# Splitting parked weights in a two-layer decoder kernel: the low half computed on GpSimd, not on VectorE

## The chip, the cores and the metric

The kernel runs on one NeuronCore of one Trainium2 chip. The core has TensorE (PE, matrix products), VectorE (DVE), ScalarE (ACT), GpSimd (POOL) and the queue engine SyncE (SP), which issues every DMA of this program. The metric is device time in microseconds of one execution, lower is better. The median of three executions of the kernel before is 1376.49 us (1376.41 to 1377.57).

## The reference, cut to what matters

The input is one sequence of 1024 rows with 1024 columns, float32. The first layer is differential attention with 8 heads, the second stick-breaking attention with 16 heads of 64, whose K and V come from a projection of their own:

```python
def reference(x, a_norm, a_w_in, a_w_out, ..., kv_norm, w_kv, b_norm, b_w_in, b_w_out):
    x = _diff_layer(x, pos, a_norm[0], a_w_in[0], a_w_out[0], ...)   # rms norm, q k v g, softmax - lam*softmax,
                                                                     # norm, times silu(g), out projection, plus x
    shared_k, shared_v = _shared_kv(x, kv_norm, w_kv)                # _rms(x, kv_norm) @ w_kv
    return _sb_layer(x, shared_k, shared_v, b_norm[0], b_w_in[0], b_w_out[0])  # _rms(x, b_norm) @ w_in, attention,
                                                                               # times silu(g), @ w_out, plus x

def _rms(x, g):
    y = x * lax.rsqrt(jnp.mean(x * x, axis=-1, keepdims=True) + RMS_EPS)
    return y * g
```

The factors `g` of the norms ahead of the second layer (`kv_norm`, `b_norm`) belong to rows of `w_kv` and `b_w_in`, so the kernel multiplies them into these weights.

## The kernel before, in words

**Products of halves.** Every float32 operand of a product is split into a high half (the value rounded to the matmul's fp32r type) and a low half (value minus high half). A product is then three matmuls: high by high, high by low, low by high. So each weight tile of 128 by 512 has to be split once on the chip: ACT copies it to the high half `h`, and an engine subtracts `h` from the value to get `l`.

**First layer.** The projections for the 8 heads run one head ahead of their attention. For every head the weights `w_qk` and `w_vg` are loaded in eight pieces of 128 by 512 into tiles called `raw`, and split into tiles called `w` (`split_w`, L519). PE multiplies (`proj`). The q and k rows go through ACT (`qk`), a norm on DVE, the rotary embedding on POOL (four instructions on `g1k` and `qk`, L1007), transposes on PE (`tr`), and a split into `q`, `qz`, `kh`, `kl`. Scores (`sc`) are evacuated by DVE to `z`, the softmax is ACT's exponentials and two passes of DVE over `z`, PE transposes the result, and ACT and DVE split it into `th` and `tl` for the product with `v` (`av`). In the last block of a row of blocks, POOL first clears a part of `th` and `tl` (L690). The gate's SiLU uses POOL twice: a bound from below on `g2k` (L610), for which ACT's exponential waits, and a product (L614). At the end come the output projection, whose weights `a_w_out` also pass through `raw` tiles, and the norm's sum of squares, also through `raw`.

**Parking.** In the same layer, spread over the steps of heads 0 to 6 (`extra`, L1195), the second layer's weights are split ahead of time and written to DRAM: 32 tiles of `w_kv`, 32 of `w_b` (both with their norm's factor `gain`) and 16 of `b_w_out` (none). That is `park` (L540): load to `raw`, `h` by ACT, `l` by DVE in place over `raw`, and two DMAs out. The second layer reads the halves back and splits no weights.

**One pool of four.** `raw` has four buffers. Parked tiles (two each, `raw` and `h`), head weights, output weights and sums of squares all take them, strictly in the order in which the code asks for them.

**What sets the order.** Nothing is issued as the code runs. Every operation is recorded, and a planner (`Order.issue`, L271) then lays out one order for all engines from a table of costs (`Order.cost`, L240), priorities and free buffers. An operation under `later()` has a low priority, one under `hp()` the highest. Each engine and the DMA queue of SP then work strictly in that order. All recorded operations carry the line L377 in the profile, so rows are told apart by tile names. The table gives a POOL operation on n columns 0.1 + 0.0028 n, a DVE `scalar_tensor_tensor` 0.12 + 0.00103 n.

Of the kernel before, what the change touches and what calls it, by code (L numbers as in the profile page):

```python
# [17 lines left out]
ALU = mybir.AluOpType  # L18
# [14 lines left out]
def f32(ap):  # L33
    return ap.bitcast(F32)
# [345 lines left out]
def build(tc, ins, out):  # L380
    nc = tc.nc
    rec = Order(tc, {"pe": nc.tensor, "act": nc.scalar, "dve": nc.vector, "pool": nc.gpsimd, "sp": nc.sync})
    act, dve, pool, pe, sp = (rec.engine(e) for e in ("act", "dve", "pool", "pe", "sp"))
# [22 lines left out]
    def later():  # L406
        return rec.priority(B["late"])
# [9 lines left out]
    def T(tag, shape, bufs, dt=F32, pool=None):  # L417
        n_t[0] += 1
        pool, name = pool or "sb", f"{tag}_{n_t[0]}"
        return L(Root(shape, dt, "psum" if pool == "ps" else "sbuf", pool, slot=(pool, tag), bufs=bufs,  # L420
                      make=lambda: pools[pool].tile(shape, dt, tag=tag, bufs=bufs, name=name)))
# [118 lines left out]
    def park(src, gain, dst):  # L540

        with later():
            raw = T("raw", [P, HALF], B["raw"], pool=layer[0])
            h = T("raw", [P, HALF], B["raw"], pool=layer[0]).bitcast(F32R)
            l = raw.bitcast(F32R)
            sp.dma_start(raw, src)
            if gain is None:
                act.activation(h, raw, AF.Copy)
                dve.tensor_tensor(l, raw, f32(h), ALU.subtract)
            else:  # L550
                act.activation(h, raw, AF.Copy, scale=gain)
                dve.scalar_tensor_tensor(l, raw, gain, f32(h), ALU.mult, ALU.subtract)
            for i, t in enumerate((f32(h), raw)):
                sp.dma_start(dst(i), t.rearrange("p (j n) -> p j n", j=2))

# [640 lines left out]
    for p2 in range(4):  # L1196
        for w, dst, c0 in ((w_kv, w2_kv, 16), (w_b, w2_b, 8)):
            for kc in range(KC):
                extra.append(lambda w=w, dst=dst, c0=c0, p2=p2, kc=kc: park(
                    w[p2, kc], cols[:, c0 + kc:c0 + kc + 1],  # L1200
                    lambda i: dst[2 * p2:2 * p2 + 2, i, :, kc * 256:(kc + 1) * 256].rearrange("j p n -> p j n")))
    for c in range(4):
        for g in range(4):
            extra.append(lambda c=c, g=g: park(
                ins["b_w_out"][c, g], None,
                lambda i: w2_o[c, i, :, g * 512:(g + 1) * 512].rearrange("p (j n) -> p j n", j=2)))
# [166 lines left out]
```

## Time and profile before

| | us |
|---|---|
| median of three executions | 1376.49 |
| the profiled execution | 1375.14 |
| its span (first to last instruction) | 1373.4 |
| first layer with parking | about 60 to 590 |
| PE, DVE, ACT, POOL busy in the span | 1334.1, 1134.5, 937.6, 349.6 |

The profiled execution is one run with the hardware's profiler, its own time 1.7 us over its span and 1.35 us under the median of the runs. In rows that group instructions, the form is `out<-in`, the shape out and in, how many, then the busy time, the mean of one in nanoseconds, and the engine's idle time before them with what ended it. PEld is PE's weight load. "SPq" is an issue by SP; its duration is that of the issue, not of the transfer.

### The profile page before, as it was taken

The page shows a single profiled execution, that of the slowest core. Times are in us where ns is not written, and L with a number is a line of the kernel's source. Part 1 is how long each engine was busy: PE and PEld are TensorE (multiplying, and loading weights), DVE is VectorE, ACT ScalarE, POOL GpSimd, SP SyncE. Part 2 cuts the span into 40 slices and gives each one's busy share as a digit, 9 for nine tenths or more (in the row PEclk, how much of TensorE's full clock was granted, in tenths as well). Part 3 has the DMA queues.
Part 4 walks back from the last instruction along what each step waited for, and adds up shares of the span by engine and source line. Part 5 has one row for each costly group of instructions (what it writes and reads, how often), then busy time and mean ns, then how long its engine had stood idle before and what let it go on. Part 6 is the DMA issues. An engine that isn't in the chain of part 4 may idle for free.

```text
span 1373.4 us, 22565 instructions
## 1 busy us (share of the span) xinstructions
PE 1334.1 (97%) x7776; PEld 1161.6 (85%) x7776; DVE 1134.5 (83%) x2079; ACT 937.6 (68%) x1830; POOL 349.6 (25%) x595
## 2 busy tenths in 40 slices
PE   8999999999999999999999999999999999999898
PEld 7998989898988888888788888888888888888677
DVE  7699899989998999976654889898989898989771
ACT  7586767676777676634435779887878788876730
POOL 5423222231312232202201124141414141424100
PEclk9999999999999999999999999999999999999999
DMA  5256656556564656862523213131322222266524
GB/s 193 78 162 191 187 160 206 171 151 195 169 207 140 198 161 178 281 233 85 177 77 130 78 64 106 62 107 63 100 70 92 78 92 78 75 201 238 192 89 141
DMA packets 104514, 194.19 MB, mean 141 GB/s; under 512 B 9936, under 2 KB 44496, under 8 KB 103376
## 3 DMA queue, kind: packets, MB, share of 16 engines
q1 hardware_dynamic: 104400, 192.75, 43.7%
q8 instruction: 62, 1.02, 0.3%
q14 instruction: 52, 0.43, 0.1%
HBM read 119.31 MB, written 65.01 MB: 134 GB/s over the span
## 4 chain that ended last, share of the span: by engine, by line
PE 61%; DVE 21%; ACT 10%; DMA 4%; issue 3%; POOL 1%; SPq 0%; DVEq 0%; ACTq 0%; POOLq 0%
PE proj L377 42%; PE av L377 7%; PE tr L377 7%; DVE z L377 5%; PE sc L377 5%; DVE u4k L377 4%; ACT u4k L377 2%; DVE tl L377 2%; ACT zl L377 1%; DVE w L377 1%; ACT qz L377 1%; DVE raw L377 1%; ACT z L377 1%; DVE v L377 1%; DVE o L377 1%
## 5 line engine op out<-in xcount | busy, mean ns | idle before, releaser
L377 PE MATMUL proj<-ah,w 128*128 128x512 f32 x2016 | 694.5, 399 | 5.2 <-DVE ah L377 2.1
L377 PEld LDWEIGHTS proj<-ah,w 128*128 128x128 f32 x2016 | 379.1, 188 | 82.5 <-DVE w L377 2.4
L377 PE MATMUL proj<-al,w 128*128 128x512 f32 x1008 | 394.9, 392 | 0.2 <-DVE al L377 0.2
L377 PEld LDWEIGHTS proj<-al,w 128*128 128x128 f32 x1008 | 190.2, 189 | 29.9 <-DVE al L377 0.5
L377 PE MATMUL proj<-w,ah 128*128 128x256 f32 x1024 | 195.7, 289 | 1.6 <-ACT ah L377 0.7
L377 DVE TENSOR_TENSOR_SCAN u4k<-zl,u4k 128x768 f32<-128x768 f32 (+4 forms) x96 | 176.3, 1837 | 3.0
L377 ACT ACTIVATE u4k<-u4k 128x768 f32<-128x768 f32 (+4 forms) x192 | 158.1, 844 | 18.0 <-DVE u4k L377 15.8
L377 PEld LDWEIGHTS proj<-w,ah 128*128 128x128 f32 x1024 | 161.6, 192 | 3.7 <-ACT ah L377 0.9
L377 DVE TENSOR_TENSOR tl<-tr,th 128x512 fp32r<-128x512 f32 (+1 forms) x240 | 145.1, 629 | 22.4 <-ACT th L377 18.6
L377 PE MATMUL av<-th,v 128*128 128x256 f32 x640 | 147.0, 284 | 3.3 <-ACT th L377 2.4
L377 PE MATMUL proj<-w,al 128*128 128x256 f32 x512 | 146.0, 285 | 3.4 <-DVE al L377 3.3
L377 ACT ACTIVATE th<-tr 128x512 fp32r<-128x512 f32 (+1 forms) x240 | 125.6, 553 | 22.1 <-PE tr L377 12.4
L377 PE MATMUL av<-tl,v 128*128 128x256 f32 x480 | 128.7, 289 | 11.1 <-DVE tl L377 10.7
L377 ACT ACTIVATE z<-z,min 128x256 f32<-128x256 f32 (+7 forms) x128 | 98.6, 771 | 59.8 <-DVE min L377 59.5
L377 POOL TENSOR_TENSOR o<-o,o 128x512 f32<-128x512 f32 (+1 forms) x56 | 85.9, 1534 | 172.0 <-DVE o L377 169.3
L377 PEld LDWEIGHTS av<-th,v 128*128 128x128 f32 x640 | 111.9, 189 | 13.2 <-ACT th L377 3.6
L377 DVE CUSTOM_DVE_ANT_0 z<-sc,mask_a 128x384 f32<-128x384 f32 (+3 forms) x192 | 102.8, 550 | 14.3 <-PE tr L377 7.5
L377 DVE SCALAR_TENSOR_TENSOR u4k<-zl,u4k 128x768 f32<-128x768 f32 (+4 forms) x96 | 96.2, 1002 | 19.3 <-ACT u4k L377 18.8
L377 PEld LDWEIGHTS av<-tl,v 128*128 128x128 f32 x480 | 90.8, 189 | 21.6 <-DVE tl L377 11.3
L377 PEld LDWEIGHTS proj<-w,al 128*128 128x128 f32 x512 | 98.1, 192 | 4.8 <-DVE al L377 4.8
L377 ACT ACTIVATE zl<-u4k 128x768 f32<-128x768 f32 (+4 forms) x96 | 81.5, 849 | 30.0 <-DVE u4k L377 29.8
L377 ACT ACTIVATE zl<-sc 128x384 f32<-128x384 f32 (+3 forms) x192 | 82.8, 494 | 20.9 <-PE sc L377 17.1
(145 smaller groups left out, 2238.6 us busy)
## 6 DMA issues: line engine op xcount, KB each, us to landing
w_kv<-raw SPq DMA_DIRECT2D x64, 256.0 KB, 2.5
w_b<-raw SPq DMA_DIRECT2D x64, 256.0 KB, 2.6
w<-w_kv SPq DMA_DIRECT2D x32, 512.0 KB, 5.3
w<-w_b SPq DMA_DIRECT2D x32, 512.0 KB, 5.0
w<-w_o SPq DMA_DIRECT2D x24, 512.0 KB, 4.9
q<-qz SPq DMA_DIRECT2D x64, 128.0 KB, 2.3
raw<-in_w_kv_dram SPq DMA_DIRECT2D x32, 256.0 KB, 2.9
raw<-in_w_b_dram SPq DMA_DIRECT2D x32, 256.0 KB, 3.0
```

The source lines that it names most:

```text
L377: getattr(e, method)(*[real(x) for x in a], **{k: real(v) for k, v in kw.items()})
```

## The change

In `park`, the subtraction moves from DVE to POOL. For a tile without a factor that is one instruction for one. For a tile with a factor, one DVE instruction (times `gain`, minus `h`) becomes two on POOL: `raw` times `gain` in place, which must wait until ACT has read `raw` for `h`, and then minus `h`, in place again.

```diff
@@ -546,10 +546,10 @@
             sp.dma_start(raw, src)
             if gain is None:
                 act.activation(h, raw, AF.Copy)
-                dve.tensor_tensor(l, raw, f32(h), ALU.subtract)
             else:
                 act.activation(h, raw, AF.Copy, scale=gain)
-                dve.scalar_tensor_tensor(l, raw, gain, f32(h), ALU.mult, ALU.subtract)
+                pool.tensor_scalar(raw, raw, gain, None, ALU.mult)
+            pool.tensor_tensor(l, raw, f32(h), ALU.subtract)
             for i, t in enumerate((f32(h), raw)):
                 sp.dma_start(dst(i), t.rearrange("p (j n) -> p j n", j=2))
```

The planner sees other costs and other engines, so it lays out the first layer anew: the order of every engine differs from the first parked tile to the output projection. In the second layer the order is the same, apart from buffer numbers.

POOL before, around the second rotary embedding of the third head (`g1k`, `qk`), with the clearing of `th` and `tl`, a gate product (`o`) and a gate bound (`g2k`) behind it:

```order
L377 TENSOR_TENSOR g1k_424_2308<-qk_381_2033,rs_93 128x16x8 x2
L377 TENSOR_TENSOR qk_381_2033<-qk_381_2033,rc_92 128x16x16
L377 TENSOR_TENSOR qk_381_2033<-qk_381_2033,g1k_424_2308 128x16x16
L377 MEMSET th_451_2394 128x128
L377 MEMSET tl_452_2412 128x128
L377 TENSOR_TENSOR o_304_2289<-o_304_2289,o_287_1624 128x512
L377 MEMSET th_498_2566 128x128
L377 TENSOR_SCALAR g2k_490_2550<-g2k_490_2550 128x512
```

POOL now, at the same place (`raw<-raw,cols` is the product with the factor, `raw<-raw,raw` the subtraction):

```order
L377 TENSOR_TENSOR raw_394_2164<-raw_394_2164,raw_395_2220 128x512
L377 TENSOR_SCALAR raw_414_2233<-raw_414_2233,cols_87 128x512
L377 TENSOR_TENSOR g1k_424_2303<-qk_381_2035,rs_93 128x16x8 x2
L377 TENSOR_TENSOR qk_381_2035<-qk_381_2035,rc_92 128x16x16
L377 TENSOR_TENSOR qk_381_2035<-qk_381_2035,g1k_424_2303 128x16x16
L377 TENSOR_TENSOR raw_414_2233<-raw_414_2233,raw_415_2274 128x512
L377 MEMSET th_451_2392 128x128
L377 TENSOR_SCALAR raw_442_2367<-raw_442_2367,cols_87 128x512
L377 MEMSET tl_452_2445 128x128
L377 TENSOR_TENSOR raw_442_2367<-raw_442_2367,raw_443_2416 128x512
L377 TENSOR_SCALAR raw_456_2419<-raw_456_2419,cols_87 128x512
L377 TENSOR_TENSOR raw_456_2419<-raw_456_2419,raw_457_2451 128x512
```

Instructions on parked tiles now stand directly ahead of the rotary embedding and of each clearing. Over the layer that holds for 11 of 16 rotary embeddings, 27 of 64 clearings and 6 of 16 gate bounds.

SP before, at the first loads of the output projection's weights (`raw<-in_a_w_out`) and of its other operand (`ah`, `al<-og_a`), in head 7:

```order
L377 DMA raw_1456_7144<-in_a_w_out_dram 128x512
L377 DMA raw_1457_7157<-in_a_w_out_dram 128x512
L377 DMA raw_1462_7209<-in_a_w_out_dram 128x512
L377 DMA raw_1463_7223<-in_a_w_out_dram 128x512
L377 DMA raw_1464_7247<-in_a_w_out_dram 128x512
L377 DMA w2_o_97<-raw_1434_6967 128x512
L377 DMA qk_1523_7254<-in_x_dram 128x2x512
L377 DMA og_a_84<-o_1293_6434 128x512
L377 DMA q0_1447_7270<-qz00_78 64x512
L377 DMA q1_1448_7277<-qz01_79 64x512
L377 DMA og_a_84<-o_1308_6926 128x512
L377 DMA raw_1465_7293<-in_a_w_out_dram 128x512
```

SP now, at the same place:

```order
L377 DMA raw_1454_7334<-in_a_w_out_dram 128x512
L377 DMA ah_1505_7350<-og_a_84 128x3072
L377 DMA al_1506_7353<-og_a_84 128x3072
L377 DMA w2_o_97<-raw_1435_7332 128x512
L377 DMA ah_1505_7350<-og_a_84 128x512
L377 DMA raw_1455_7377<-in_a_w_out_dram 128x512
L377 DMA kh_1520_7379<-in_x_dram 128x2x512
L377 DMA w2_o_97<-raw_1434_7243 128x512
L377 DMA al_1506_7353<-og_a_84 128x512
L377 DMA kl_1521_7425<-in_x_dram 128x2x512
L377 DMA raw_1456_7429<-in_a_w_out_dram 128x512
L377 DMA raw_1457_7501<-in_a_w_out_dram 128x512
```

Before, all eight weight loads (`raw_1454` to `raw_1465`) are issued ahead of `ah` and `al`; now one is, and seven come behind these two large loads.

## Rows read from the trace of the kernel before

**Rows 1.** The page: busy time, share of the span, instructions by engine.

```profile
PE 1334.1 (97%) x7776; PEld 1161.6 (85%) x7776; DVE 1134.5 (83%) x2079; ACT 937.6 (68%) x1830; POOL 349.6 (25%) x595
```

**Rows 2.** Stretches: length, busy PE, PEld, DVE, ACT, POOL; clock, DMA share, GB/s.

```profile
60.00:580.00 520.00, 508.40 (x3327) 457.64 (x3326) 476.74 (x1146) 360.30 (x793) 132.61 (x172) 1.00 0.58 180
580.00:700.00 120.00, 117.05 (x570) 96.15 (x568) 77.05 (x168) 47.70 (x92) 21.66 (x22) 1.00 0.50 171
```

**Rows 3.** Waits of PE, 60 to 580: us in total, times, longest.

```profile
PE av L377 <- DVE tl L377: 4.7, 5, 1.6
PE av L377 <- ACT th L377: 2.4, 6, 1.2
PE sc L377 <- DVE min L377: 1.5, 2, 1.1
```

**Rows 4.** Waits of PE's weight loads, 60 to 580.

```profile
PEld sc L377 <- DVE min L377: 5.0, 11, 1.3
PEld av L377 <- POOL o L377: 4.9, 4, 1.8
...
PEld tr L377 <- POOL qk L377: 3.6, 8, 0.6
```

**Rows 5.** Groups of DVE instructions by form, 60 to 590.

```profile
L377 DVE SCALAR_TENSOR_TENSOR raw<-raw,cols,raw 128x512 fp32r<-128x512 f32 x64 | 54.7, 862 | 3.7 <-ACT raw L377 3.4
...
L377 DVE TENSOR_TENSOR w<-raw,w 128x512 fp32r<-128x512 f32 x61 | 45.5, 769 | 2.0 <-ACT w L377 1.7
...
L377 DVE TENSOR_TENSOR min<-min 128x1 f32<-128x1 f32 x56 | 14.3, 256 | 1.6
...
L377 DVE TENSOR_TENSOR raw<-raw,raw 128x512 fp32r<-128x512 f32 x16 | 12.4, 780 | 0.0
```

**Rows 6.** Groups of POOL instructions by form, 60 to 590.

```profile
L377 POOL TENSOR_SCALAR g2k<-g2k 128x512 f32<-128x512 f32 x15 | 25.1, 1674 | 28.8 <-DVE g2k L377 22.8 <-ACT th L377 4.5 <-DVE sum L377 1.5
...
L377 POOL TENSOR_TENSOR o<-o,o 128x512 f32<-128x512 f32 x14 | 18.1, 1294 | 100.5 <-DVE o L377 100.5
```

**Rows 7.** Timeline of DVE, 268 to 281: start, us, engine, instruction.

```profile
271.84 0.16 DVE L377 TENSOR_TENSOR min<-min 128x1 f32<-128x1 f32 x1
...
276.61 1.22 DVE L377 TENSOR_TENSOR min<-min 128x1 f32<-128x1 f32 x1
...
279.52 0.74 DVE L377 TENSOR_SCALAR z<-z,sum 128x1024 f32<-128x1024 f32 x1
```

**Rows 8.** Timeline of POOL, 268 to 281.

```profile
276.01 1.79 POOL L377 TENSOR_TENSOR o<-g2k,o 128x512 f32<-128x512 f32 x1 [0.48 <-POOL o L377]
278.97 1.75 POOL L377 TENSOR_SCALAR g2k<-g2k 128x512 f32<-128x512 f32 x1 [1.17 <-DVE g2k L377]
```

**Rows 9.** DMA issues: queue, how many, KB each, median us to landing.

```profile
w_kv<-raw SPq DMA_DIRECT2D x64, 256.0 KB, 2.5
...
raw<-in_w_kv_dram SPq DMA_DIRECT2D x32, 256.0 KB, 2.9
...
ah<-og_a SPq DMA_DIRECT2D x1, 1536.0 KB, 8.2
```

**Rows 10.** Instructions on `raw`, whole program: durations in ns, min/median/max, then starts, forms.

```profile
L377 DVE TENSOR_TENSOR w<-raw,w x80: 678/687/1773, 52.9 to 675.9; 128x512 fp32r<-128x512 f32 x80
L377 ACT ACTIVATE raw<-raw,cols x64: 707/713/727, 69.1 to 463.2; 128x512 fp32r<-128x512 f32 x64
```

**Rows 11.** Timeline of SP's issues, 520 to 572: the first output weights.

```profile
536.14 10.63 SPq L377 DMA_DIRECT2D raw<-in_a_w_out_dram  x5
...
551.69 0.73 SPq L377 DMA_DIRECT2D ah<-og_a  x1
```

**Rows 12.** Timeline of PE, 545 to 575: the output projection's first product.

```profile
569.52 0.48 PE L377 MATMUL proj<-ah,w 128*128 128x512 f32 x1
```

**Rows 13.** Chain that ended last, 560 to 615: start, us, what.

```profile
585.39 3.92 DMA w_o<-raw
...
589.34 4.53 DMA raw<-in_a_w_out_dram
```

## The prediction

> **What bounds the kernel now.** I read the page's busy times first [rows 1]: PE 97%, DVE 83%, POOL 25%. These are means over two layers, and only the first one parks weights, so the next view is the stretches [rows 2]. From 60 to 580 us PE is busy 508.4 of 520 us, DVE 476.7 (92%), ACT 360.3, POOL 132.6 (26%). So DVE is nearly as full as PE while weights are parked, and POOL has room. But PE is idle for only 520 - 508.4 = 11.6 us of this stretch, and another 3.0 us from 580 to 700. That is the most that any relief of another engine can give back. The views of waits say whom PE waits for. PE proper waits for DVE's `tl` and `min` 4.7 + 1.5 = 6.2 us and for ACT 2.4 [rows 3]. Its weight loads wait 5.0 for `min`, and 4.9 + 3.6 = 8.5 us for POOL, though POOL is three quarters idle [rows 4]. Weight-load waits count only in part, since a matmul in front may cover them.
>
> **What goes from DVE.** 64 instructions with the factor, 54.7 us, and 16 without, 12.4 us [rows 5]: 67.1 us, 14% of DVE's time in the stretch.
>
> **What comes to POOL.** 80 subtractions of two inputs on 128x512, 1.29 us each by the nearest row, and 64 products with a factor. The trace has no POOL product with a column as factor. The nearest row is the bound on `g2k`, same shape, one input, one number, 1.67 us; the other end is below the subtraction's price, since one operand less is read, say half of it, 0.65 [rows 6]. I take 1.67, as both are the same instruction on the same shape. So 80 x 1.29 + 64 x 1.67 = 103 + 107 = 210 us (145 with the low price). POOL goes from 132.6 to some 340 us of 520, 65%.
>
> The Trainium skill ("GPSIMD Engine Reference", section 4.1) calls two-input work about twice as slow on GpSimd, which the rows show (1.29 against 0.69 on DVE, [rows 6, 10]), but one-input work roughly line rate. At its 128 values per cycle and 1.2 GHz, 512 columns would be an estimated 0.43 us; the row has 1.67, four times that. The measurement decides; by the page POOL would gain about 130 us, not 210, and the cases with a crowded POOL would weigh less.
>
> **What the two engines cost each other.** At 276.01 POOL starts a two-input instruction and ends it at 277.80; DVE's one-column `min` of that moment takes 1.22 us and ends as POOL does, where its like at 271.84 takes 0.16. But the DVE instruction of 279.52 runs its 0.74 us wholly inside POOL's `g2k` bound (278.97 to 280.72) [rows 7, 8]. So a POOL subtraction stops DVE instructions that read two tensors of SBUF, and a POOL product hardly does. Of the DVE instructions that remain, `w` and `min` show the loss: their means over their undisturbed 0.68 and 0.16 us give 61 x 0.09 + 56 x 0.10 = 11 us [rows 5, 7, 10]. For the smaller groups together I double that, by estimate, to 20. POOL's two-input time in the stretch is at most 132.6 - 25.1 = 107 us [rows 2, 6], and 103 us are added, so the loss doubles: 20 us more on DVE. Net relief of DVE 67 - 20 = 47 us, 10%.
>
> The Trainium skill ("SBUF — State Buffer", section Who interferes with whom) says more: any GpSimd instruction holds the shared port pair for its whole length, and a DVE instruction with two SBUF inputs, or in a fast two-port mode, is blocked until it ends. For two-input POOL work the trace agrees (1.22 us); the 0.74 us inside the bound does not. By the rule the 64 products would block too; this is the third rival.
>
> **What it does to PE.** (a) DVE relief: `tl` and `min` come earlier. With a tenth less work on a queue that is 92% full I take half of the 6.2 us, -3. Bounds: nothing, and the whole 6.2 + 5.0 = -11.2 (which is nearly all of PE's idle time).
>
> (b) POOL's queue. POOL works strictly in order. 11 of 16 rotary embeddings, 27 of 64 clearings and 6 of 16 gate bounds now stand directly behind an instruction on a parked tile, as the order of POOL shows; the product of each pair waits for ACT's `h`, and the subtraction for the product. Queued behind are the transposes of q and k (they wait for `qk`), the `av` products (for the clearing of `th`), and ACT's exponential (for `g2k`). Where POOL is late, each is late by up to one instruction, 1.3 to 1.7 us. Half of that, 0.75, on 11 embeddings and some 14 pairs of clearings is 19 us of lateness. PE has projections of the next head to fill with, but in a fixed order. Today 8.5 us of weight-load waits for POOL sit beside 11.6 us of idle time, so a quarter to a third reaches PE: +5. Bounds: 0 and 19.
>
> (c) The `raw` buffers. Undisturbed, a parked tile holds its `raw` buffer for load 2.9, ACT 0.72, DVE 0.86, store 2.5 = 7.0 us, and the one for `h` for 4.1 [rows 5, 9, 10]; with 1.67 + 1.29 for 0.86, both rise by 2.1. Over 64 + 16 tiles (0.5 for those without a factor) that is 64 x 4.2 + 16 x 1.0 = 285 buffer-us, on four buffers 71 us of a stretch of 524. The four are handed out in a fixed order, so head weights and output weights queue behind parked tiles. The place where this bites is the output projection. Before, its first eight weight loads are all issued ahead of `ah` (551.69, 8.2 us to land), for a first product at 569.5 [rows 9, 11, 12]: 18 us or more in hand. Now seven of the eight come behind `ah` and `al` on SP, in part after the 0.5 MB loads of `kh` and `kl`. In hand are then only a few us, and the splits, which have priority on ACT, crowd the last head's `th`. The chain near 590 already runs through a `w_o` store of 3.9 and an `a_w_out` load of 4.5 us [rows 13]: one such round late is what I allow, +4. Bounds: 0 and two to three rounds more, 15.
>
> **Sum.** -3 + 5 + 4 = +6 us on the profiled execution's 1375.1, so 1381. This execution stands 1.35 us below the median of the runs; I take 1382 as the forecast. SP carries the same DMAs as before. The second layer keeps its order, and its weights are in DRAM long before it starts, so nothing changes there.
>
> **Rivals.** First, faster: DVE is the one that PE waits for, and POOL's lateness is hidden by projections. Then (a) is -6 to -11 and (b) and (c) together 2 at most: 1367 to 1373, say 1371. For it: DVE at 92% and the rows on `tl` and `min`. Against it: POOL's waits in rows 4 at only 26% load, and the 11.6 us of ceiling. It decides once (b) and (c) stay under 4 us.
>
> Second, no change: PE's own work of 508 us in 520 sets the pace, and (a) cancels (b) and (c): 1374 to 1379. For it: the small idle time at both ends. Against it: new waits can add without a ceiling while removed ones cannot.
>
> Third, the product on POOL blocks DVE after all: 64 products, with two of five DVE moments sensitive at 0.8 us or more, so nearly each product stops one instruction: 50 us back on DVE, (a) goes to 0 and the lateness of (b) grows by some 2: 1387.
>
> Fourth, the `raw` buffers run dry: of the 71 us of four buffers that (c) adds, a fifth is not absorbed by the waits that they stand in today, and PE starves in head 7 and the output projection by 10 to 20 us: 1387 to 1397 with (a) and (b), say 1393. For it: seven loads moved back, and the earlier slack of only 18 us. Against it: with weights already late, their tiles no longer sit in `raw` waiting for a free `w`, so the pool recovers.
>
> **How the numbers follow.** Forecast (1379.5 to 1386) 0.38, faster 0.28, no change 0.20, blocking 0.06, starving 0.08. A measurement of this kernel can tell about 0.2%, 2.75 us, from no change: faster is then 0.28, same 0.20, slower 0.38 + 0.06 + 0.08 = 0.52. The range from 1370 to 1394 leaves out a tenth on the side of starving and the best end of the first rival; the forecast's own range is 1379.5 to 1386.
>
> **What would show it.** Right: DVE's busy time from 60 to 580 falls by 40 to 50 us, POOL's rises by about 200; the new POOL rows read about 1.3 and 1.7 us; PE's waits for DVE shrink by about half and those for POOL (`av`, `tr`) grow; the idle time of PE from 560 to 600 grows by some us, with `a_w_out` loads or ACT's `w` at its end. Wrong: PE's idle time in the stretch falls below 8 us (the first rival), or `w` and `min` rise to more than twice their means (the third), or PE waits for `w` in heads 5 to 7 (the fourth).

## The result and the profile after

The changed kernel takes 1401.53 us (median of four runs, 1401.28 to 1402.68), the kernel before beside it 1377.03 us: a ratio of 1.0184 (95% interval 1.0171 to 1.0197). Slower was forecast, but 1382; 1401.5 lies outside the range. The profiled execution takes 1402.68 us with a span of 1400.8, 27.4 us over the span before.

The page's busy times, to be held against [rows 1]:

```profile
PE 1349.5 (96%) x7776; PEld 1169.3 (83%) x7776; DVE 1119.9 (80%) x1999; ACT 940.2 (67%) x1830; POOL 561.3 (40%) x739
```

POOL has 211.7 us more, as forecast (210). DVE lost 80 instructions of 67.1 us [rows 5] but only 14.6 us of busy time. So the instructions that stayed became 52.5 us longer in sum, where the forecast had 20.

Stretches, columns as in [rows 2], of the parking and of the last head with the output projection:

```profile
60.00:580.00 520.00, 499.83 (x3233) 445.90 (x3232) 444.50 (x1029) 350.42 (x762) 333.52 (x306) 0.99 0.56 171
...
600.00:620.00 20.00, 14.37 (x78) 11.89 (x77) 14.45 (x29) 6.02 (x13) 7.97 (x10) 0.94 0.88 321
620.00:640.00 20.00, 18.67 (x67) 13.46 (x66) 17.40 (x47) 10.64 (x21) 0.00 (x0) 0.72 0.32 101
```

PE is idle for 20.2 us of the first stretch, where it was 11.6. From 600 to 640 it was busy 38.6 us before at full clock; now it is busy 33.0, and the granted clock falls to 0.72 from 620 to 640.

Two milestones say where the time was lost. M1 is the start of the last head's second group of transposes of rotated rows on PE; M2 is SP's first load of a parked weight, where the second layer begins. Here are their rows, first of the kernel before, then of the changed one:

```profile
544.61 1.09 PE L377 MATMUL tr<-ident,qk 128*128 128x128 f32 x8 [0.21 <-POOL qk L377]
...
675.30 0.83 SPq L377 DMA_DIRECT2D w<-w_kv  x2
```

```profile
560.09 1.03 PE L377 MATMUL tr<-ident,qk 128*128 128x128 f32 x8
...
701.70 0.80 SPq L377 DMA_DIRECT2D w<-w_kv  x2
```

M1 is 15.5 us late, M2 26.4. So 15.5 us are lost up to the last head ("heads" below) and 10.9 behind it ("behind"). Through the second layer the 26.4 stay nearly as they are (27.4 at the end). 1.1 us of the heads' loss lies ahead of the first parked tile. Such lags come from one execution of each kernel, while the executions of the kernel before that go with these runs lie between 1374.7 and 1382.1 us: a lag under some 4 us says little.

The stretches from 60 us to M1 and from M1 to M2, first before, then changed, show in what form the time is lost:

```profile
60.00:544.61 484.61, 473.96 (x3132) 428.55 (x3130) 444.81 (x1069) 335.79 (x741) 123.39 (x161) 1.00 0.57 174
544.61:675.30 130.69, 126.80 (x647) 104.59 (x648) 101.85 (x229) 68.21 (x136) 25.69 (x30) 1.00 0.55 188
```

```profile
60.00:560.09 500.09, 481.50 (x3137) 431.27 (x3136) 428.14 (x996) 337.56 (x738) 326.09 (x299) 0.99 0.54 165
560.09:701.70 141.61, 131.83 (x649) 107.27 (x648) 104.95 (x224) 69.92 (x140) 33.86 (x36) 0.95 0.56 189
```

Up to M1 PE is idle for 18.6 us (10.7 before) and busy for 7.5 us longer with nearly the same instructions. So waits are only about half of the heads' loss. Part of the longer busy time is the clock: its granted share is 0.50 from 358 to 361 us and 0.53 from 508 to 511, each time right behind gaps in which PE waited for `tl` or `min` (2.05 us, and 1.1 + 0.4). The rest of the 7.5 us stays open. Behind M1 PE is idle 5.9 us more and busy 5.0 us longer, together the 10.9.

POOL's new groups, 60 to 610 us (form of [rows 6]), have the forecast prices, 1.69 us for the product and 1.37 for the subtraction:

```profile
L377 POOL TENSOR_SCALAR raw<-raw,cols 128x512 f32<-128x512 f32 x64 | 108.2, 1690 | 66.7 <-ACT raw L377 43.7 <-DVE w L377 11.5 <-DVE small L377 5.2
L377 POOL TENSOR_TENSOR raw<-raw,raw 128x512 fp32r<-128x512 f32 x79 | 107.8, 1365 | 28.5 <-ACT raw L377 24.6
```

PE's waits, 60 to 580 us (form of [rows 3]), show what was not forecast. For `tl` and `min` they did not halve from 6.2 us but rose to 10.8, and for `z` and `q` they are 1.9 (0.3 before). The wait for POOL's `qk` is small:

```profile
PE av L377 <- DVE tl L377: 6.3, 10, 2.0
PE sc L377 <- DVE min L377: 4.5, 6, 1.4
PE av L377 <- ACT th L377: 4.4, 5, 1.4
PE tr L377 <- POOL qk L377: 2.1, 5, 0.8
PE tr L377 <- DVE z L377: 1.0, 2, 0.6
PE tr L377 <- DVE q L377: 0.9, 2, 0.7
```

The DVE instructions that became longer are those of the softmax and the norms (groups by form, 60 to 610 us). Its two passes over `z` (`z<-z,sum` and `z<-z,sum,z`) gain 7.8 and 6.6 us over all shapes. Of the small ones `min` had a mean of 256 ns in [rows 5], `sum` and `small` 232 and 173 in this view of before:

```profile
L377 DVE TENSOR_TENSOR sum<-sum,lam 128x1 f32<-128x1 f32 x60 | 20.5, 341 | 2.0
L377 DVE TENSOR_TENSOR min<-min 128x1 f32<-128x1 f32 x56 | 19.8, 365 | 0.9
...
L377 DVE TENSOR_TENSOR small<-small,small 128x16 f32<-128x16 f32 x45 | 12.5, 278 | 2.5 <-ACT small L377 1.4
```

How one comes to be longer is seen in the timelines of POOL and of DVE (start, us, instruction; as [rows 7, 8]):

```profile
283.23 1.29 POOL L377 TENSOR_TENSOR raw<-raw,raw 128x512 fp32r<-128x512 f32 x1
...
352.02 1.29 POOL L377 TENSOR_TENSOR raw<-raw,raw 128x512 fp32r<-128x512 f32 x1
...
414.11 1.56 POOL L377 TENSOR_SCALAR raw<-raw,cols 128x512 f32<-128x512 f32 x1
```

```profile
283.40 1.13 DVE L377 TENSOR_TENSOR min<-min 128x1 f32<-128x1 f32 x1
...
352.00 1.79 DVE L377 TENSOR_SCALAR z<-z,sum 128x896 f32<-128x896 f32 x1
...
414.18 0.62 DVE L377 TENSOR_TENSOR min<-min 128x1 f32<-128x1 f32 x1
```

The subtraction ends at 284.52, the `min` at 284.53: DVE is let go when POOL's instruction ends. The same holds for all 21 instructions on `min`, `sum` and `small` that start between 0.02 and 1.14 us into a subtraction: they end 0.01 to 0.03 us after it. The pass over `z` at 352.00 takes 1.79 us beside a subtraction, its like at 269.34 in the kernel before 0.67, so an instruction that reads one tensor and one column is stopped as well. Behind it PE waits the 2.05 us for `tl`, until 357.80, and the clock falls. The product ends at 415.67, but the `min` beside it at 414.80, some 0.7 us after the product's start. So a product stops DVE too, for somewhat under half of its time.

Behind the heads SP's timeline shows the first output weights (before, the first eight were all issued by 551 us, five of them in [rows 11]):

```profile
566.18 0.40 SPq L377 DMA_DIRECT2D raw<-in_a_w_out_dram  x1
571.05 0.45 SPq L377 DMA_DIRECT2D raw<-in_a_w_out_dram  x1
579.92 6.44 SPq L377 DMA_DIRECT2D raw<-in_a_w_out_dram  x4
591.93 1.40 SPq L377 DMA_DIRECT2D raw<-in_a_w_out_dram  x2
...
606.66 0.33 SPq L377 DMA_DIRECT2D raw<-in_b_w_out_dram  x1
621.19 2.15 SPq L377 DMA_DIRECT2D raw<-in_a_w_out_dram  x4
```

The second lot, at 585 to 594 us before, comes at 621, behind the last four parked tiles. Until then PE has no projections and waits for the last head's softmax; its timeline shows the gap:

```profile
615.90 0.34 PE L377 MATMUL sc<-kh,qz 128*128 128x384 f32 x1
619.50 0.69 PE L377 MATMUL sc<-kl,q 128*128 128x384 f32 x1 [3.26 <-DVE min L377]
```

Around this gap the clock falls to the lower level of 1.2 GHz: its granted share is 0.52 from 617 to 631 us, a stretch with 10.2 us of busy time. That explains the 5.0 us by which PE is busy longer behind M1: 0.48 x 10.2 = 4.9.

### The profile page after: what moved, and what is told of

The parts are those of the page before. It is cut to its first block, busy times and chain, and to the rows that moved or that the text cites. A ratio compares the mean times of both kernels' runs of the same rounds, so it can differ in the third digit from the quotient of the medians.

```text
span 1400.8 us, 22654 instructions
## 1 busy us (share of the span) xinstructions
PE 1349.5 (96%) x7776; PEld 1169.3 (83%) x7776; DVE 1119.9 (80%) x1999; ACT 940.2 (67%) x1830; POOL 561.3 (40%) x739
## 4 chain that ended last, share of the span: by engine, by line
PE 59%; DVE 24%; ACT 9%; issue 3%; DMA 3%; POOL 1%; SPq 0%; ACTq 0%; DVEq 0%; POOLq 0%
PE proj L377 40%; DVE z L377 7%; PE av L377 7%; PE tr L377 7%; PE sc L377 5%; DVE u4k L377 4%; DVE tl L377 2%; ACT u4k L377 2%; ACT z L377 2%; DVE w L377 1%; ACT zl L377 1%; DVE sum L377 1%; DVE o L377 1%; DVE small L377 1%; DVE min L377 1%
## 5 line engine op out<-in xcount | busy, mean ns | idle before, releaser
L377 PE MATMUL proj<-w,ah 128*128 128x256 f32 x1024 | 198.7, 292 | 1.5 <-ACT ah L377 0.7
L377 PEld LDWEIGHTS proj<-w,ah 128*128 128x128 f32 x1024 | 165.0, 196 | 3.6 <-ACT ah L377 0.9
L377 POOL TENSOR_SCALAR raw<-raw,cols 128x512 f32<-128x512 f32 x64 | 108.2, 1690 | 66.7 <-ACT raw L377 43.7
L377 PEld LDWEIGHTS av<-th,v 128*128 128x128 f32 x640 | 111.3, 189 | 15.5 <-ACT th L377 4.8
L377 POOL TENSOR_TENSOR raw<-raw,raw 128x512 fp32r<-128x512 f32 x80 | 109.5, 1369 | 35.0 <-ACT raw L377 31.0
L377 POOL TENSOR_SCALAR_AFFINE_SELECT zl<-zl 128x128 f32<-128x128 f32 (+1 forms) x96 | 57.8, 616 | 116.3 <-ACT zl L377 115.9
```

What stands on the lines that cost most here:

```text
L377: getattr(e, method)(*[real(x) for x in a], **{k: real(v) for k, v in kw.items()})
```

## The experiments

Theory A: POOL's two-input instructions stop DVE instructions that PE waits for. Theory B: POOL's own lateness in its strict order. Theory C: the planner's new order and the `raw` buffers. The expectations of the runs letter their own theories anew. Twelve kernels were run. Where an edit says "emit", the planner lays out the order for the recorded operation, and other instructions are issued in its place (the lines that do this are not shown). These kernels have a line more, so their rows read L378. "Heads" is the lag of M1 against the trace before, "behind" that of M2 less that of M1:

| label | us | ratio (95%) | heads | behind |
|---|---|---|---|---|
| after | 1401.53 | 1.0184 (1.0171 to 1.0197) | +15.5 | +10.9 |
| e1_old_order | 1441.61 | 1.0457 (1.0436 to 1.0477) | +64.2 | +0.3 |
| e2_new_order | 1389.95 | 1.0080 (1.0061 to 1.0099) | +7.3 | +8.3 |
| e3_one_input | 1381.93 | 1.0023 (1.0012 to 1.0034) | -2.7 | +8.0 |
| e4_raw6_after | 1399.20 | 1.0147 (1.0128 to 1.0166) | +23.8 | -1.0 |
| e5_raw6_before | 1381.55 | 1.0031 (1.0021 to 1.0042) | +3.3 | +1.9 |
| e6_four_pieces | 1390.35 | 1.0099 (1.0084 to 1.0114) | +6.8 | +7.0 |
| e7_only_wo | 1380.15 | 1.0019 (1.0007 to 1.0032) | +4.6 | -2.0 |
| e8_not_wo | 1396.59 | 1.0142 (1.0127 to 1.0157) | +11.3 | +8.1 |
| e9_six_heads | 1409.27 | 1.0238 (1.0221 to 1.0255) | +34.6 | -3.6 |
| e10_six_before | 1378.08 | 1.0010 (0.9996 to 1.0023) | +3.8 | -1.6 |
| e11_six_pieces | 1403.45 | 1.0193 (1.0175 to 1.0211) | +33.1 | -3.3 |
| e12_six_one_input | 1397.07 | 1.0150 (1.0131 to 1.0170) | +23.5 | -4.8 |

**The old order with POOL's work (e1).** Planned as before, POOL issues the product and the subtraction where DVE had its one instruction.

```diff
                 dve.scalar_tensor_tensor(l, raw, gain, f32(h), ALU.mult, ALU.subtract)
+            times = [] if gain is None else [("tensor_scalar", (raw, raw, gain, None, ALU.mult), {})]
+            rec.ops[-1].emit = ("pool", times + [("tensor_tensor", (l, raw, f32(h), ALU.subtract), {})])
```

> The planner lays out the order of the kernel before (it is told that the low half is made on VectorE), but the instructions themselves go to GpSimd, at the same place among all instructions. Theory A, the work on GpSimd itself (its longer latency, its in-order queue and the VectorE instructions that it stops) costs the time: 1394 us or more, since the order is not adapted to the later low halves either. Theory B, the order that the planner made for the new costs is the poorer one: 1374 to 1382 us. Half and half: 1385 to 1391.

1441.61, far above the 1394 of the expectation. Here theory B is seen, in the waits of PE from 60 to 610 us:

```profile
PE tr L378 <- POOL qk L378: 31.7, 10, 5.9
PE av L378 <- DVE tl L378: 8.9, 11, 1.4
```

The rotary embeddings stand behind parked tiles, and PE waits 31.7 us for them. In the changed kernel that is 2.1 us: its order has made room, and with POOL's work this order saves 64.2 - 15.5 = 48.7 us in the heads. The next run prices it with DVE's work. Behind the heads e1 loses only 0.3 us, late as its heads are.

**The new order with DVE's work (e2).**

```diff
                 pool.tensor_scalar(raw, raw, gain, None, ALU.mult)
+                rec.ops[-1].emit = ("pool", [])
             pool.tensor_tensor(l, raw, f32(h), ALU.subtract)
+            rec.ops[-1].emit = ("dve", [("tensor_tensor", (l, raw, f32(h), ALU.subtract), {}) if gain is None else
+                                        ("scalar_tensor_tensor", (l, raw, gain, f32(h), ALU.mult, ALU.subtract), {})])
```

> The reverse: the order of the changed kernel, but the low half is one VectorE instruction again, at the place of the GpSimd subtraction, and the product on GpSimd is left away. Theory A (the work on GpSimd): 1376 to 1384 us. Theory B (the order): 1394 to 1402, as the changed kernel. If the output projection's late weights come from the order alone, its part, some 11 of the 25 us, stays: 1387 to 1391.

1389.95, within the third of its ranges: with every instruction still on its engine the changed order costs 7.3 us in the heads and 8.3 behind them. The forecast had no such term for the heads. The planner made this order for POOL's work, so DVE's instructions stand where it took DVE to be free; what a poorer order and what this mismatch costs is not separated. The page's busy times, and then the groups of the parked tiles on DVE (by form, 60 to 610 us):

```profile
PE 1342.2 (97%) x7776; PEld 1164.2 (84%) x7776; DVE 1127.2 (81%) x2079; ACT 940.9 (68%) x1830; POOL 350.1 (25%) x595
```

```profile
L378 DVE SCALAR_TENSOR_TENSOR raw<-raw,cols,raw 128x512 fp32r<-128x512 f32 x64 | 50.9, 795 | 0.1
...
L378 DVE TENSOR_TENSOR raw<-raw,raw 128x512 fp32r<-128x512 f32 x16 | 10.9, 683 | 0.5 <-ACT raw L378 0.5
```

**One input instead of two (e3).** In the changed order, the 80 subtractions become products of one input (`h` times zero), so the parked low halves are zero.

```diff
             pool.tensor_tensor(l, raw, f32(h), ALU.subtract)
+            rec.ops[-1].emit = ("pool", [("tensor_scalar", (l, f32(h), 0.0, None, ALU.mult), {})])
```

> The changed kernel and its order, but the 80 subtractions of two inputs on GpSimd are replaced by 80 products of one input (h times 0, so the parked low halves are zero). GpSimd is busy some 20 us longer, with no second input. If VectorE loses because two-input work on GpSimd stops its instructions, the waits of TensorE for VectorE in heads 1 to 7 go back and 10 us or more are won: 1386 to 1392. If it is the latency of the pair, the queue or the order: 1399 to 1405.

1381.93, below the expected 1386 to 1392. POOL is no less busy than in the changed kernel (353.8 us against 333.5 from 60 to 580), yet the heads come 18.2 us earlier. That speaks for theory A and against B. Against e2, with the same order, DVE's relief, less what the products and POOL's lateness take from it, is worth 10.0 us. The page's busy times:

```profile
PE 1342.6 (97%) x7776; PEld 1167.2 (85%) x7776; DVE 1098.1 (80%) x1999; ACT 941.1 (68%) x1830; POOL 579.4 (42%) x739
```

In e2 DVE was busy for 1127.2 us; less the 61.8 of its parked tiles that is 1065.4. So 144 one-input products cost DVE 32.7 us, 0.23 each, while the changed kernel's 64 products and 80 subtractions cost 54.5. At 0.23 for a product, a subtraction takes (54.5 - 14.5) / 80 = 0.50 us from DVE. The products let DVE go early, as these timelines show, POOL's and then DVE's:

```profile
251.35 1.50 POOL L378 TENSOR_SCALAR raw<-raw 128x512 fp32r<-128x512 f32 x1
...
475.33 1.57 POOL L378 TENSOR_SCALAR raw<-raw,cols 128x512 f32<-128x512 f32 x1 [2.13 <-ACT raw L378]
```

```profile
251.43 0.56 DVE L378 TENSOR_TENSOR min<-min 128x1 f32<-128x1 f32 x1
...
475.60 0.43 DVE L378 TENSOR_TENSOR min<-min 128x1 f32<-128x1 f32 x1
```

Both `min` end 0.64 to 0.70 us after the start of a product that lasts 1.5 us or more.

**Four pieces (e6).** The same subtraction in four instructions of 128 columns, so that DVE gets in between.

```diff
+            rec.ops[-1].emit = ("pool", [("tensor_tensor", (l[:, c:c + 128], raw[:, c:c + 128],
+                                                            f32(h)[:, c:c + 128], ALU.subtract), {})
+                                         for c in range(0, 512, 128)])
```

> The changed kernel's order; each of the 80 subtractions on POOL is cut into four instructions of 128 columns, same result. Theory A (a DVE instruction that comes during a POOL subtraction waits for the end of that one instruction, so the length of one counts): one piece lasts about a third to a quarter of 1.3 us, DVE gets in between, and of the some 18 us that the subtractions cost the heads (changed kernel against the one-input version) at least half goes: 1386 to 1392 us. Rival B (the total time of two-input work counts, not its pieces): POOL's total rises by the four fixed costs, so no gain: 1400 or more. Rival C (POOL's own lateness was the cost): four pieces are longer in sum, so slower: above 1404.

1390.35. POOL's subtractions last 155.7 us in place of 109.5, and still the heads come 8.7 us earlier:

```profile
L378 POOL TENSOR_TENSOR raw<-raw,raw 128x128 fp32r<-128x128 f32 x320 | 155.7, 517 | 28.1 <-ACT raw L378 23.7 <-DMA w_o<-raw 0.5
```

So the length of one blocking instruction counts, not POOL's total: theory A, as expected. About half of the 18.2 us goes. PE's wait for `qk` rises to 3.5 us here, so part of what remains may be POOL's lateness; that split stays open.

**One part alone (e7, e8).** Only the 16 tiles without a factor on POOL, and only the 64 with one.

```diff
             if gain is None:
                 act.activation(h, raw, AF.Copy)
-                dve.tensor_tensor(l, raw, f32(h), ALU.subtract)
+                pool.tensor_tensor(l, raw, f32(h), ALU.subtract)      # e7: this alone
             else:
                 act.activation(h, raw, AF.Copy, scale=gain)
-                dve.scalar_tensor_tensor(l, raw, gain, f32(h), ALU.mult, ALU.subtract)
+                pool.tensor_scalar(raw, raw, gain, None, ALU.mult)    # e8: these two alone
+                pool.tensor_tensor(l, raw, f32(h), ALU.subtract)
```

> Only the 16 tiles without a factor (b_w_out, the last parked, from about 463 us on) are subtracted on POOL; the 64 with a factor stay on DVE in one instruction; planned anew. Theory A (the heads lose where POOL subtracts; the end loses 8 to 11 us because the last parked tiles hold raw buffers longer just ahead of the output weights): heads lag only in head 6 and 7, by up to 5 us, the stretch behind them by 5 to 10: 1383 to 1392. Rival B (the end is late because the heads are late, not by the last parks): end within 2 us of before, 1377 to 1382.

> The other part alone: the 64 tiles with a factor on POOL in two instructions, the 16 without stay on DVE; planned anew. Theory A: the heads are late as in the changed kernel until head 6 (10 to 15 us), but the output weights are loaded as early as before and the end adds 0 to 3 us: 1387 to 1395. Rival B (end late because of the heads): end adds 8 to 11 here too, 1397 to 1402.

For the end, theory A of these two expectations fell: the last 16 tiles cost nothing behind the heads on POOL (-2.0), and 8.1 us are lost with those tiles on DVE. e7's time lies in the rival's range, e8's, 1396.59, between the two. The rival's numbers behind the heads came, but late heads alone are not the reason, since e1 has the latest heads and loses 0.3. What goes with the loss is that the row of parked tiles runs later than the heads: the first load of `b_w_out` starts at 461.5 us before, 462.9 in e7, 495.5 in e8 and 496.8 in the changed kernel, although the heads of the changed kernel are only some 12 us late there. In e2 and e3, at 491.9 and 484.0, it is some 23 us later than the heads too; in e1, at 518.8, it is about as late as they are.

**Six raw buffers (e4, e5).** The changed kernel and the one before, with room made by a pair of padded q tiles less. Some scores then read the q of the next head, so these two do not compute the reference; the work of each engine is the same.

```diff
-    B = {..., "raw": 4, ..., "qz": 3, ...}
+    B = {..., "raw": 6, ..., "qz": 2, ...}
```

> The changed kernel with six raw buffers in place of four (the room comes from the padded q tiles, two pairs in place of three), laid out anew. If the raw buffers are what starves the output projection, and in part the heads, 11 us or more are won: 1380 to 1391 us. If they only seem to, within 4 us of the changed kernel: 1397 to 1405.

> The kernel before with six raw buffers and two padded q pairs instead of three (with two, some scores read the q of the next head; the work per engine is the same). It is the like of the run with six raw buffers that had the changed split (heads +23.8, end -1.0 against before). Theory A (that run's late heads come from the q pairs and the two-input blocking, its good end from the buffers): here heads +5 to +12, end -3 to 0: 1380 to 1390. Rival B (six buffers cost the heads nothing, the changed split is all of it): heads within 3 us of before, 1374 to 1380.

Each against the like of it, the change costs 20.5 us in the heads with six buffers (23.8 - 3.3; e5's +3.3 lies between its two theories) and nothing behind them (-1.0 - 1.9). The first output weights are loaded at 530.5 us, where the kernel before has 528.6, and the clock stays at full level from M1 to 688 us. So the loss behind the heads goes with the `raw` buffers. The heads' loss is not cured by them, and by its time alone e4, at 1399.20, is the rival of its expectation.

**Parked tiles over six heads (e9 to e12).** So that they are done ahead of the output weights: the changed kernel, the kernel before, the four pieces, and the one-input products.

```diff
-            main = spread(main, extra[h * len(extra) // (n - 1):(h + 1) * len(extra) // (n - 1)])
+            main = spread(main, extra[h * len(extra) // (n - 2):(h + 1) * len(extra) // (n - 2)])
```

> The changed kernel with its 80 parked tiles spread over heads 0 to 5 instead of 0 to 6; planned anew. Theory A (the 11 us behind the heads come from parked tiles that stand ahead of the output weights in the one pool of raw buffers, run late, and leave PE without projections and at half clock near 620): the output weights are asked for earlier, PE is at full clock from 580 to 660, the stretch behind the heads adds 0 to 4 us; the heads lose 0 to 8 us more, since parked work is denser: 1392 to 1402. Rival B (the end is late for another reason, the last head's own softmax): the end still adds 8 to 11 and the half clock stays: 1401 to 1410.

> The like of it without the change: the kernel before with its parked tiles spread over six heads; planned anew. Theory A: its end has nothing to gain, its heads get denser: 1376 to 1384. Rival B: the same. Its use is the difference to the changed kernel spread alike: theory A says that this difference is 12 to 20 us, as the two-input blocking and the order alone; rival B 22 to 28.

> Both remedies: the changed kernel with the parked tiles over six heads and each subtraction in four instructions of 128 columns. Theory A: the savings of the two add up, heads about +6 to +10 against before, end 0 to 4: 1380 to 1390, still not below the kernel before. Rival B (the pieces' longer POOL time is in the way where parked work is denser): no better than with four pieces over seven heads: 1390 to 1398.

> The changed kernel with its parked tiles over six heads, and each subtraction on POOL replaced by a one-input product (the other operand times zero), so that the second layer's weights have low halves of zero; order as with six heads. In question is why the heads became 19 us later there (group 15 at +34.6 against before) than with seven heads (+15.5). Theory A (blocking of DVE by two-input instructions, in denser parked work): most of the 34.6 goes, heads at 0 to +8, time 1373 to 1383. Rival B (parked tiles hold the raw buffers too long, head weights come late, whoever does the work): the one-input instruction is no shorter, so heads stay at +18 or more, time 1392 or more.

Behind the heads the theory A of these expectations was right in all of them: -1.6 to -4.8, and in e9 PE works at full clock through the stretch in which it starved:

```profile
600.00:620.00 20.00, 20.00 (x112) 17.31 (x110) 18.07 (x47) 13.19 (x33) 4.85 (x9) 1.00 0.47 152
620.00:640.00 20.00, 20.00 (x99) 16.98 (x98) 10.22 (x29) 3.31 (x7) 0.35 (x2) 1.00 0.50 198
```

In the heads it was wrong. e9 is 34.6 us late, not 15 to 23, while the kernel before takes the denser parking for 3.8; the difference of the two times, 31.2 us, fits neither theory. The pieces gain 1.5 us, not some 9, and e11's time lies outside both its ranges. One input in place of two frees 11.1 us of the 34.6 and leaves 23.5, so by its numbers the rival in e12 is right for the larger part. Its reason, that parked tiles which stay longer in `raw` hold up the heads' own weights, is argued more than shown: PE waits for those only 4.0 us (waits of e9, 60 to 650 us; 0.6 before):

```profile
PE proj L377 <- DVE w L377: 4.0, 4, 1.7
```

How much of the 23.5 us is the buffers themselves and how much the order that the planner lays out around them was not separated. The clock has a part in e9: its granted share is 0.50 from 320 to 330, from 402 to 408 and from 525 to 528 us, and up to M1 PE is busy 16.1 us longer than before. No version with parked work on POOL beats the kernel before; the nearest, e7, is 0.2% slower.

## Why the prediction was wrong, point by point

**What held.** The direction; the prices of POOL's instructions and its sum (211.7 us against 210); SP's late output weights; that the second layer adds almost nothing.

**The step that failed** is "What the two engines cost each other", and with it term (a). I doubled the loss of 11 us that `w` and `min` showed, "by estimate, to 20", because POOL's two-input time doubled. The loss is 52.5 us by the two profiles, so the net relief of DVE is not 47 us but 15. By e2 and e3 the subtractions take 40 us where 20 was put, and the products 14.5 where nothing was. I also took the relief as a mean: a tenth less work on DVE, so half of PE's waits for it. But what is blocked are the softmax's instructions, those of one column and the passes over `z`, which stand in the chain to PE. And the forecast priced waits alone, where about half of the heads' loss is PE's own longer busy time, in part at the lower clock. In the same order, relief alone is worth 10.0 us (e2 to e3, POOL's own lateness included), and the two-input blocking costs 18.2 (e3 to the changed kernel). So (a) came out at +8.2 and not -3.

**The product.** I excluded blocking by products from one DVE instruction, a pass over `z` that began 0.55 us after the start of the bound on `g2k`. It could show little: a product lets DVE go after some 0.7 us, of which 0.15 were left. Nor does the number of tensors read tell what is stopped, since a subtraction stops a pass of this kind (352.00). The third rival was right in kind, but at 0.23 us for each product, not 0.8.

The Trainium skill ("SBUF — State Buffer", section Who interferes with whom) says that whoever issues first holds the shared port pair for its whole instruction and blocks the other; for DVE instructions with two inputs it names GpSimd instructions that read SBUF, and not any, as my forecast put it. For the subtraction the trace agrees (284.52 and 284.53); for the product, which reads SBUF as well, the block ends 0.7 us into 1.56, and the measurement decides. The same skill ("Perfetto Trace Analysis", section Optimizing Scalar/DVE Operations) warns that moving work between these two engines might not help; the 54.5 us that came back to DVE agree.

**(b), POOL's queue, +5.** Wrong in place. In the changed kernel PE's waits for `qk` rose by 1.3 us only, since the planner knows that POOL is slow and has laid out another order (e1 shows 31.7 us of them without it). That order costs 7.3 us in the heads with DVE's work (e2). The sum needed this as a term of its own: I read from the order what stands behind what, but priced only the waits.

**(c), the buffers, +4 (bounds 0 and 15).** Right in place, sized too small: 10.9 us. The mechanism is right in part: the order in which the buffers are handed out brings 8.3 by itself, with the work back on DVE (e2), and the 2.6 that are left are within the scatter of executions. I allowed for one late round of store and load. But the last sixteen parked tiles are loaded 35 us late, some 23 more than the heads, so the second lot of output weights is late too, and then the lower clock nearly doubles the price of the idle time (5.0 us on 5.9). It comes with the 64 tiles with a factor (e8), which have most of the 285 buffer-us in (c).

**The sum, by the runs:** heads +7.3 (order) - 10.0 (relief) + 18.2 (blocking) = +15.5; behind +8.3 (order) + 2.6 = +10.9; together 26.4 of the span's 27.4. These parts follow one path, from the kernel before over e2 and e3. Over e1 the heads would split into +64.2 for POOL's work in the old order and -48.7 for the new order, so the parts are not properties of the change alone.

## What to carry to other kernels

Before moving work from VectorE to GpSimd, multiply GpSimd's new instructions by what each takes from VectorE (0.50 us for a two-input subtraction of 512 columns here, 0.23 for a one-input product), and ask whether the instructions that it stops lie in the chain that TensorE waits for. Where a planner lays out the order, run the new order with the old instructions: what it pays ahead for a slow engine does not show as a wait for that engine. A row of work that runs late in a shared pool of buffers is paid where the next user of the pool stands, here the output weights. A gap on TensorE can cost clock as well, so count its busy time too and not only its waits.

## What the runs showed of the hardware

- A two-input DVE instruction of one column (0.16 us undisturbed, [rows 7]) ends 0.01 to 0.03 us after the POOL subtraction that it met, up to 1.1 us late. Beside a one-input POOL product it ends 0.64 to 0.70 us after the product's start. A pass over `z`, which reads one tensor and one column, is stopped by a subtraction too (1.79 us for 0.67).
- The one-input product of 128x512 on POOL takes longer than the two-input subtraction (1.69 and 1.37 us), yet takes less than half as much from DVE (0.23 and 0.50).
- A subtraction of 128 columns on POOL takes 0.52 us, one of 512 columns 1.37: some 0.23 us of each are fixed, by an estimate from these means, (4 x 0.517 - 1.365) / 3.
- From M1 to M2 PE was idle 5.9 us more and busy 5.0 us longer for nearly the same instructions, with a granted clock of 0.52 from 617 to 631 us around a gap of 3.26 us. Behind a gap of 2.05 us its granted clock was 0.50 from 358 to 361 us.
